# Five weight places in the second sweep, first projections back to back, fetched rows' products last in a unit

## The chip, the cores and the metric

The kernel runs on one core of one Trainium2 chip. The metric is the device time of one execution in microseconds; before the change the median of three runs is 1904.34 us (1901.85 to 1908.06).

## What is computed

One decoder block over 256 tokens of width 2048, in float32, with one layer:

```
h  = RMSNorm(x);  z = h @ w_in          # split into q, k, v, c_q, c_kv, k_r, gate_a, gate_b
y_a = window attention(q, k, v) @ w_a   # 16 heads, window 128
y_b = latent attention(c_q, c_kv, k_r) @ w_b
x  = x + (sigmoid(gate_a) * y_a + sigmoid(gate_b) * y_b) @ w_o
h2 = RMSNorm(x)
# expert mixer: per token 8 heads x 16 of 16384 experts, chosen by top-k of key scores
a  = h2 . u[expert];  w = gelu(a) * gate;  x = x + sum of w * v[expert]
out = RMSNorm(x)
```

`u` and `v` are tables of 16384 rows of 2048 floats (128 MB each).

## The kernel before

**Weights as pieces.** All weights, in the order in which they are used, are cut into pieces of at most 2048 floats per partition (1 MB); `plan` lists them, with `u` and `v` as the last 128 pieces each. `feed_hi` (L100) takes the next piece: it gets a place `raw` (three of them, in turn), lets SP start the transfer (L107), and lets ACT copy it to float32r, a rounded form (`whi`, L108). The function that it returns lets DVE make the remainder (`wlo` = `raw` - `whi`, L112). Two places each of `whi` and `wlo` follow. A matrix product is then summed on PE from the parts: high by high, high by low, low by high. `stream` keeps one piece ahead. SP issues its transfers in order, each when its `raw` place has been released by L112.

**Order of the work.** Up to the second sweep's beginning, a scheduler at compile time fills the engines' queues from the program and its dependences, so an instruction can stand earlier in a queue than it does in the program (POOL clears `vap`, L417, at 1.57 us). From `tc.manual_schedule()` (L945) on, the program's order is each engine's order.

**The start.** x is transposed and loaded in four parts; `make_x` (L206) makes `xc`, the high and low parts of x times gain, by ACT and DVE, one of 16 column blocks after the other. `nblock` (L159) multiplies row-wise: for every k three matmuls for each of two token halves. First comes `c_q` (512 columns, 96 matmuls, L242), with `make_x` called in groups of four blocks by `ahead_x`; then the norm of x: eight squares with sums on ACT (L248), a chain of small steps for `r1c`, two multiplications by the identity (`dg`, L255), and two products with ones on PE (L256), whose copy is `r1`. Then `c_kv` with `k_r` (320 columns, 96 matmuls, L376), written out with the factor `r1c` by `rows_out`.

**The u sweep.** Tokens are split: 192 (TD) get all 16384 experts by dense products, 64 (TG) get only their 128 experts each, whose rows are fetched. Per unit j of 128 (L948): 16 matmuls with `whi` (L952), in some units four products of one-hot matrices for the gates (L958, 48 such groups), then 16 matmuls with `wlo` (L981). Meanwhile ACT copies the last unit's PSUM (L902), makes the next `whi`, and applies GELU; DVE multiplies finished rows by their gates (L962), adds the PSUM parts (L905), makes the next `wlo` (L112), multiplies gate blocks (L979) and makes one-hots (L940).

**Fetched rows.** `gathered` (L844) is a generator of 130 steps. A step of the first 64 lets POOL fetch 128 rows of `u` by index (an indirect DMA of 1 MB, L828) into one of two places `urow`, and lets DVE multiply the row before by `h_nat` and sum it (L852, 2048 elements). Then one step for GELU, and 64 steps that fetch rows of `v` into three places `vrow` and add them, weighted, into `h_nat` (L865). A fetch waits until the product that read its place is done. `gather_to(goal)` runs steps up to a number: 54 (GU) of them are spread over the units of the u sweep after the routing is done (unit JR), the other 76 over the v sweep.

**The v sweep (the second sweep of 128 pieces).** For every piece n (L1036): 12 matmuls with `whi` (L1050 to L1052) and 8 with `wlo` (L1033), all 512 columns wide, into the eight PSUM banks, from stationary columns `wc` that ACT and DVE prepare for two pieces at a time (L873, L875, L876). `take(1)` at its top feeds the next piece, so that its `wlo` stands on DVE ahead of the step of `gathered` at the bottom. In pieces 80 to 103 SP also loads x and the last gain in 12 parts of 256 KB (L1044).

Of the kernel before, what the change touches and what calls it, by code (L numbers as in the profile page):

```python
# [8 lines left out]
F32 = mybir.dt.float32  # L9
# [56 lines left out]
def block(tc, a, out):  # L66
# [23 lines left out]

    plan, fed, ready = [], [0], []
    AHEAD = 1

    def planned(src):
# [3 lines left out]
    def feed_hi():  # L100
        src = plan[fed[0]]
        per, cols = src.shape[1], src.shape[2]
        m = per * cols
        raw = ring.tile([P, 2048], F32, name="raw", bufs=3)[:, :m]
        hi = ring.tile([P, 2048], F32R, name="whi", bufs=2)[:, :m]
        lo = ring.tile([P, 2048], F32R, name="wlo", bufs=2)[:, :m]
        sync.dma_start(raw.rearrange("p (k c) -> p k c", k=per), src)  # L107
        act.activation(hi, raw, AF.Copy)  # L108
        fed[0] += 1

        def rest():
            vec.tensor_tensor(lo, raw, hi.bitcast(F32), op=OP.subtract)  # L112
            ready.append([(hi[:, k * cols:(k + 1) * cols], lo[:, k * cols:(k + 1) * cols]) for k in range(per)])

        return rest
# [42 lines left out]

    def nblock(pss, nk, act_c, ahead=None):  # L159
        for k in range(nk):  # L160
            if ahead and k % 4 == 0:
                ahead(k // 4)
            wh, wl = next(wts)
            for c, ps in enumerate(pss):
                cs = slice(c * P, (c + 1) * P)
                pe.matmul(ps, act_c[:, k, 0, cs], wh, start=k == 0, stop=False)  # L166
                pe.matmul(ps, act_c[:, k, 0, cs], wl, start=False, stop=False)  # L167
                pe.matmul(ps, act_c[:, k, 1, cs], wh, start=False, stop=k == nk - 1)  # L168
# [19 lines left out]
    def acc_tile():  # L188
        accs[0] += 1
        return ps_acc.tile([P, 512], F32, name="acc", bufs=4)  # L190
# [12 lines left out]
    def load_x(k0, k1):  # L203
        sync.dma_start(xT[:, k0:k1, :], a["xT"][:, k0:k1, :])

    def make_x(k0, k1):  # L206
        for k in range(k0, k1):
            act.activation(xc[:, k, 0], xT[:, k], AF.Copy, scale=gm[:, k:k + 1])
            vec.scalar_tensor_tensor(xc[:, k, 1], xT[:, k], gm[:, k:k + 1], xc[:, k, 0].bitcast(F32),
                                     op0=OP.mult, op1=OP.subtract)  # L210
# [4 lines left out]
    ss = s0.tile([P, 2], F32, name="ss")  # L215
    tmp1 = s0.tile([P, 2], F32, name="tmp1")

    def ahead_x(q):
        if q == 0:
            return  # L220
        if q < 3:
            make_x(4 * q + 4, 4 * q + 8)


    idle = s0.tile([P, 512], mybir.dt.bfloat16, name="idle")
# [8 lines left out]
    make_x(2, 4)  # L234
    feed_hi()()
    load_x(4, 8)
    make_x(4, 8)
    feed_hi()()
    load_x(8, 12)
    load_x(12, 16)  # L240
    pss_cq = [acc_tile() for _ in range(2)]
    nblock(pss_cq, KO, xc, ahead=ahead_x)  # L242
    for c in range(2):
        sync.dma_start(xn[:, c], a["x_rows"][c])
    for c in range(2):
        for i in range(4):
            d = slice(i * 512, (i + 1) * 512)
            act.activation(xn[:, c, d], xn[:, c, d], AF.Square, accum_out=sp4[:, c, i:i + 1])  # L248
    vec.tensor_reduce(ss, sp4, axis=AX.X, op=OP.add)
    vec.tensor_scalar(ss, ss, 1.0 / D, EPS, op0=OP.mult, op1=OP.add)  # L250
    rsqrt(r1c, ss, tmp1)
    dg = s0.tile([P, 2, P], F32, name="dg")
    ps = acc_tile()
    for c in range(2):
        vec.tensor_scalar(dg[:, c], ident, r1c[:, c:c + 1], None, op0=OP.mult)  # L255
        pe.matmul(ps[:, c * P:(c + 1) * P], ones, dg[:, c], start=True, stop=True)  # L256
    act.activation(r1, ps[:, :T], AF.Copy)
    st.close()


# [79 lines left out]
    def rows_proj(cols, dst):  # L340
        pss = [acc_tile() for _ in range(2)]
        nblock([p[:, :cols] for p in pss], KO, xc)
        rows_out(dst, pss, cols)
# [29 lines left out]
                                     op0=OP.mult, op1=OP.mult)  # L373

    rows_out(cq, pss_cq, 512)
    rows_proj(320, ckr)  # L376
    norm_rows(cq, 512, gcq)
    norm_rows(ckr, 256, gckv)
    for c in range(2):
# [507 lines left out]
    def gather_to(goal):  # L887
        nonlocal gdone
        while gdone < STEPS and gdone <= goal:
            next(gat, None)  # L890
            gdone += 1
# [56 lines left out]
    for j in range(NJ):  # L948
        ps = acc_tile()
        ws = ready.pop(0)  # L950
        for k, (wh, wl) in enumerate(ws):
            pe.matmul(ps[:, :2 * TD], wh, hc[:, k].rearrange("p a t -> p (a t)"), start=k == 0, stop=False)  # L952
        fresh = []
        if hot and hot[0][0] + 2 <= j:
            G = ps_g.tile([P, 4, P], F32, name="G", bufs=2)
            _, o1, o2 = hot.pop(0)
            for q in range(4):
                pe.matmul(G[:, q], o1[:, q], o2[:, q], start=True, stop=True)  # L958
            fresh.append(G)
        while prods:  # L960
            bj, ge = prods.pop(0)
            vec.tensor_tensor(bj, bj, ge, op=OP.mult)  # L962
        add = evict(*last) if last else None
        ready_lo = feed_hi()
        old = gelus[:]
        gelus.clear()
        if add:
            add()
        work.pull(1.5)
        if JR is not None:  # L970
            gather_to((j - JR) * GU / (NJ - JR))
        rest = []
        while grids:
            rest += finish_gates(grids.pop(0))
        for g in old:
            finish_unit(*g)
        ready_lo()
        for bh, gv in rest:
            vec.tensor_tensor(bh, bh, gv, op=OP.mult)  # L979
        for k, (wh, wl) in enumerate(ws):  # L980
            pe.matmul(ps[:, :TD], wl, hc[:, k, 0], start=False, stop=k == KO - 1)  # L981
        last = (j, ps)
        grids += fresh
        if j == 0:
            scores(*behind)
            work.add(routing())
            qs.close()
            xs.close()
            b1 = bs.enter_context(tc.tile_pool(name="b1", bufs=1))
            B.append(b1.tile([P, NJ // 2, TD], F32, name="B0"))  # L990
        if JR is None and not work.gens:
            JR = j
            rt.close()
            b2 = bs.enter_context(tc.tile_pool(name="b2", bufs=1))
            B.append(b2.tile([P, NJ // 2, TD], F32, name="B1"))
            ps_g = hs.enter_context(tc.tile_pool(name="ps_g", bufs=1, space=PSUM))
        if JR is None:
            continue
        if groups < NG and groups * (NJ - 8 - JR) < (j + 1 - JR) * NG:
            hot.append((j, *one_hots(4 * groups)))  # L1000
            groups += 1
        if j == NJ - 2:
            assert not grids
            assert done == TD and not hot
            gs.close()
            wcp = bs.enter_context(tc.tile_pool(name="wcp", bufs=1, reuse_waits="tile"))
            wcs = [take_w(0)]
# [28 lines left out]
    for n in range(NJ - 2):  # L1036
# [16 lines left out]
        add_to(0, S[:1], vl, turn=accs[0])  # L1053
        add_to(1, S[2:], vl, turn=accs[0])
        gather_to(GU + (n + 1) * (STEPS - GU) / (NJ - 8))
        if n == NJ - 5:
            assert gdone == STEPS
            act.activation(x2[LO, 3], h_nat[HI], AF.Copy)
            vec.tensor_tensor(x2[LO, 1], x2[LO, 1], h_nat[LO], op=OP.add)
# [149 lines left out]
```

## Time and profile before

| | before |
|---|---|
| median of three runs | 1904.34 us |
| profiled execution | 1913.5 us |
| its span, first to last instruction | 1911.7 us |
| PE busy | 1870.5 us (98%) |
| DVE busy | 1593.1 us (83%) |
| ACT busy | 1139.8 us (60%) |
| POOL busy | 349.9 us (18%) |
| moved by DMA | 526.16 MB, mean 275 GB/s |

PE is TensorE's matmul side, PEld its weight loads, DVE is VectorE, ACT is ScalarE, POOL is GpSimd, SP is the engine whose queue starts most transfers. A busy share counts the time in which an instruction of the engine runs. Matmuls overlap, so PE's busy time is not PE at its peak. The profiled execution is one, and its own time is 1913.5 us; the runs of the median were made without a profile.

### The profile page before, as it was taken

The numbers are of one execution on the slowest core, as the hardware profiler recorded it, in microseconds if no ns is written. First come the engines' busy times: TensorE is split into PE (matmuls) and PEld (weight loads), VectorE is DVE, ScalarE is ACT, GpSimd is POOL, SyncE is SP. The second block draws the span as 40 slices with busy tenths as digits, with TensorE's granted clock in tenths as the row PEclk, the third lists the DMA queues.
The fourth block names the chain that finished last, engine by engine and source line by source line (L and its number), as shares of the span: only waits on it lengthen the run. The fifth ranks groups of instructions, "written<-read, shape, count | busy, mean of one in ns | idle before, by whom it ended". The sixth has DMA issues, their size and how long they took to land.

```text
span 1911.7 us, 28123 instructions
## 1 busy us (share of the span) xinstructions
PE 1870.5 (98%) x10874; PEld 1680.9 (88%) x10874; DVE 1593.1 (83%) x2277; ACT 1139.8 (60%) x1754; POOL 349.9 (18%) x192
## 2 busy tenths in 40 slices
PE   8999999999999999999999999999999999999996
PEld 6888888888888999999999999998788788887885
DVE  5768878658679799998899999998888898888887
ACT  7655766545555455555999998855444444444444
POOL 0000000000000000515243334333322123112210
PEclk9999999999999999999999999999999999999998
DMA  7554444455555566667798898889999999999983
GB/s 275 191 174 151 143 162 141 160 192 180 207 203 185 176 216 231 227 229 274 295 346 345 345 350 338 324 335 356 373 374 359 386 385 364 387 395 381 399 328 127
DMA packets 77910, 526.16 MB, mean 275 GB/s; under 512 B 9168, under 2 KB 11472, under 8 KB 15568
## 3 DMA queue, kind: packets, MB, share of 16 engines
q1 hardware_dynamic: 59344, 390.14, 56.6%
q0 software_dynamic: 18432, 134.23, 17.3%
q8 instruction: 85, 1.39, 0.3%
q14 instruction: 49, 0.40, 0.1%
HBM read 520.14 MB, written 4.19 MB: 274 GB/s over the span
## 4 chain that ended last, share of the span: by engine, by line
PE 60%; issue 16%; POOL 8%; DVE 6%; DMA 5%; ACT 5%; SPq 0%; POOLq 0%; DVEq 0%; ACTq 0%
PE acc L146 15%; PE o L1033 8%; PE acc L952 8%; POOL urow L828 8%; PE acc L151 7%; PE acc L981 5%; PE o L1050 4%; DMA raw<-v 4%; PE o L1052 4%; PE o L1051 4%; DVE wlo L112 3%; ACT whi L108 3%; PE acc L167 1%; PE acc L168 1%; PE acc L166 1%
## 5 line engine op out<-in xcount | busy, mean ns | idle before, releaser
L112 DVE TENSOR_TENSOR wlo<-raw,whi 128x2048 fp32r<-128x2048 f32 (+2 forms) x363 | 827.0, 2279 | 216.4 <-ACT whi L108 212.7
L108 ACT ACTIVATE whi<-raw 128x2048 fp32r<-128x2048 f32 (+2 forms) x363 | 688.6, 1897 | 450.3 <-DMA raw<-v 238.9
L952 PE MATMUL acc<-hc,whi 128*128 128x384 f32 x2048 | 382.8, 339 | 0.0
L952 PEld LDWEIGHTS acc<-hc,whi 128*128 128x128 f32 x2048 | 353.2, 189 | 0.0
L981 PE MATMUL acc<-hc,wlo 128*128 128x192 f32 x2048 | 252.9, 275 | 4.8 <-DVE wlo L112 4.8
L1033 PE MATMUL o<-wlo,wc 128*128 128x512 f32 x1020 | 252.5, 390 | 1.5 <-DVE wlo L112 1.5
L981 PEld LDWEIGHTS acc<-hc,wlo 128*128 128x128 f32 x2048 | 244.8, 193 | 6.3 <-DVE wlo L112 6.3
L1033 PEld LDWEIGHTS o<-wlo,wc 128*128 128x128 f32 x1020 | 191.0, 188 | 42.6 <-DVE wlo L112 2.9
L146 PE MATMUL acc<-xc,whi 128*128 128x512 f32 x928 | 227.6, 394 | 0.0
L828 POOL DMA_INDIRECT urow<-u_rows,iv x64 | 167.0, 2610 | 314.1 <-DVE urow L852 311.1
L1050 PE MATMUL o<-whi,wc 128*128 128x512 f32 x504 | 197.5, 392 | 4.3 <-ACT whi L108 3.8
L146 PEld LDWEIGHTS acc<-xc,whi 128*128 128x128 f32 x928 | 170.3, 189 | 32.1
L1051 PE MATMUL o<-whi,wc 128*128 128x512 f32 x504 | 196.2, 389 | 0.0
L1052 PE MATMUL o<-whi,wc 128*128 128x512 f32 x504 | 196.2, 389 | 0.0
L828 POOL DMA_INDIRECT vrow<-v_rows,iv x64 | 116.1, 1814 | 347.3 <-DVE h_nat L865 317.3
L852 DVE SCALAR_TENSOR_TENSOR urow<-urow,h_nat 128x2048 f32<-128x2048 f32 x64 | 146.2, 2285 | 21.9 <-DMA urow<-u_rows,iv 21.9
L865 DVE SCALAR_TENSOR_TENSOR h_nat<-vrow,gg,h_nat 128x2048 f32<-128x2048 f32 x63 | 147.8, 2346 | 0.0
L721 POOL TENSOR_TENSOR cand<-tv 128x256 f32<-128x256 f32 x16 | 14.0, 891 | 730.4 <-DVE tv L714 633.4
L902 ACT ACTIVATE ge<-acc 128x192 f32<-128x192 f32 x128 | 41.4, 324 | 152.7 <-PE acc L981 150.4
L151 PEld LDWEIGHTS acc<-xc,wlo 128*128 128x128 f32 x928 | 119.2, 191 | 4.5
L151 PE MATMUL acc<-xc,wlo 128*128 128x256 f32 x928 | 121.2, 283 | 0.0
L1050 PEld LDWEIGHTS o<-whi,wc 128*128 128x128 f32 x504 | 94.6, 188 | 28.5 <-ACT whi L108 8.3
(329 smaller groups left out, 2254.8 us busy)
## 6 DMA issues: line engine op xcount, KB each, us to landing
raw<-u SPq DMA_DIRECT2D x128, 1024.0 KB, 5.1
raw<-v SPq DMA_DIRECT2D x128, 1024.0 KB, 8.2
raw<-w_ga SPq DMA_DIRECT2D x16, 1024.0 KB, 4.8
raw<-w_gb SPq DMA_DIRECT2D x16, 1024.0 KB, 4.8
raw<-w_o SPq DMA_DIRECT2D x16, 1024.0 KB, 4.9
raw<-w_pq SPq DMA_DIRECT2D x16, 1024.0 KB, 4.9
raw<-w_q SPq DMA_DIRECT2D x8, 1024.0 KB, 4.8
raw<-w_a SPq DMA_DIRECT2D x8, 1024.0 KB, 4.9
```

The lines of the kernel that those rows point to most:

```text
L108: act.activation(hi, raw, AF.Copy)
L112: vec.tensor_tensor(lo, raw, hi.bitcast(F32), op=OP.subtract)
L146: pe.matmul(ps, ws[k][0], act_c[:, k].rearrange("p a t -> p (a t)"), start=k == 0, stop=False)
L151: pe.matmul(ps[:, :T], ws[k][1], act_c[:, k, 0], start=False, stop=k == nk - 1)
L828: pool.indirect_dma_start(out=dst, out_offset=None, in_=table, in_offset=bass.IndirectOffsetOnAxis(ap=idx, axis=0))
L865: later(vec.scalar_tensor_tensor(h_nat, r, gg[:, i:i + 1], h_nat, op0=OP.mult, op1=OP.add))
L952: pe.matmul(ps[:, :2 * TD], wh, hc[:, k].rearrange("p a t -> p (a t)"), start=k == 0, stop=False)
L981: pe.matmul(ps[:, :TD], wl, hc[:, k, 0], start=False, stop=k == KO - 1)
L1033: pe.matmul(O[c][i], st_, v[:, i * 512:(i + 1) * 512], start=first and k == 0, stop=last and k == len(ss) - 1)
L1050: pe.matmul(O[0][i], S[0], vh[:, d], start=n == 0, stop=False)
L1051: pe.matmul(O[0][i], S[1], vh[:, d], start=False, stop=False)
L1052: pe.matmul(O[1][i], S[2], vh[:, d], start=n == 0, stop=False)
```

## The change

It does four things. In the start, `ahead_x` makes one column block of `xc` ahead of every k instead of four ahead of every fourth; the `c_kv` product runs directly behind the `c_q` product on PE, with the squares of the norm called in two groups at its k = 4 and k = 8, and L256 comes after it, into a PSUM tile of its own. In the u sweep the step of `gathered` moves from ahead of the next `wlo` to behind it and behind the gate products, not in the last unit, with its 54 steps spread over one unit less. In the v sweep, once all 64 products with `urow` are issued (`gdone > NS`), two of every five pieces (those whose number leaves 3 or 4 when divided by 5) use the two `urow` places as their `raw`; the others go on with the three of the ring.

```diff
--- before.py
+++ after.py
@@ -90,7 +90,7 @@
 
 
 
-    plan, fed, ready = [], [0], []
+    plan, fed, ready, spare = [], [0], [], []
     AHEAD = 1
 
     def planned(src):
@@ -101,7 +101,10 @@
         src = plan[fed[0]]
         per, cols = src.shape[1], src.shape[2]
         m = per * cols
-        raw = ring.tile([P, 2048], F32, name="raw", bufs=3)[:, :m]
+        if spare and fed[0] % 5 > 2:
+            raw = spare[0]()
+        else:
+            raw = ring.tile([P, 2048], F32, name="raw", bufs=3)[:, :m]
         hi = ring.tile([P, 2048], F32R, name="whi", bufs=2)[:, :m]
         lo = ring.tile([P, 2048], F32R, name="wlo", bufs=2)[:, :m]
         sync.dma_start(raw.rearrange("p (k c) -> p k c", k=per), src)
@@ -158,8 +161,8 @@
 
     def nblock(pss, nk, act_c, ahead=None):
         for k in range(nk):
-            if ahead and k % 4 == 0:
-                ahead(k // 4)
+            if ahead:
+                ahead(k)
             wh, wl = next(wts)
             for c, ps in enumerate(pss):
                 cs = slice(c * P, (c + 1) * P)
@@ -215,11 +218,14 @@
     ss = s0.tile([P, 2], F32, name="ss")
     tmp1 = s0.tile([P, 2], F32, name="tmp1")
 
-    def ahead_x(q):
-        if q == 0:
-            return
-        if q < 3:
-            make_x(4 * q + 4, 4 * q + 8)
+    def ahead_x(k):
+        if k + 6 < KO:
+            make_x(k + 6, k + 7)
+
+    def squares_x(c):
+        for i in range(4):
+            d = slice(i * 512, (i + 1) * 512)
+            act.activation(xn[:, c, d], xn[:, c, d], AF.Square, accum_out=sp4[:, c, i:i + 1])
 
 
     idle = s0.tile([P, 512], mybir.dt.bfloat16, name="idle")
@@ -234,27 +240,29 @@
     make_x(2, 4)
     feed_hi()()
     load_x(4, 8)
-    make_x(4, 8)
+    make_x(4, 6)
     feed_hi()()
     load_x(8, 12)
     load_x(12, 16)
+
     pss_cq = [acc_tile() for _ in range(2)]
     nblock(pss_cq, KO, xc, ahead=ahead_x)
     for c in range(2):
         sync.dma_start(xn[:, c], a["x_rows"][c])
-    for c in range(2):
-        for i in range(4):
-            d = slice(i * 512, (i + 1) * 512)
-            act.activation(xn[:, c, d], xn[:, c, d], AF.Square, accum_out=sp4[:, c, i:i + 1])
+    pss_ck = [acc_tile() for _ in range(2)]
+    psn = ExitStack()
+    ps_n = psn.enter_context(tc.tile_pool(name="ps_n", bufs=1, space=PSUM))
+    nblock([p[:, :320] for p in pss_ck], KO, xc, ahead=lambda k: squares_x(k // 4 - 1) if k in (4, 8) else None)
     vec.tensor_reduce(ss, sp4, axis=AX.X, op=OP.add)
     vec.tensor_scalar(ss, ss, 1.0 / D, EPS, op0=OP.mult, op1=OP.add)
     rsqrt(r1c, ss, tmp1)
     dg = s0.tile([P, 2, P], F32, name="dg")
-    ps = acc_tile()
+    ps = ps_n.tile([P, 512], F32, name="nacc")
     for c in range(2):
         vec.tensor_scalar(dg[:, c], ident, r1c[:, c:c + 1], None, op0=OP.mult)
         pe.matmul(ps[:, c * P:(c + 1) * P], ones, dg[:, c], start=True, stop=True)
     act.activation(r1, ps[:, :T], AF.Copy)
+    psn.close()
     st.close()
 
 
@@ -373,7 +381,7 @@
                                      op0=OP.mult, op1=OP.mult)
 
     rows_out(cq, pss_cq, 512)
-    rows_proj(320, ckr)
+    rows_out(ckr, pss_ck, 320)
     norm_rows(cq, 512, gcq)
     norm_rows(ckr, 256, gckv)
     for c in range(2):
@@ -967,8 +975,6 @@
         if add:
             add()
         work.pull(1.5)
-        if JR is not None:
-            gather_to((j - JR) * GU / (NJ - JR))
         rest = []
         while grids:
             rest += finish_gates(grids.pop(0))
@@ -977,6 +983,8 @@
         ready_lo()
         for bh, gv in rest:
             vec.tensor_tensor(bh, bh, gv, op=OP.mult)
+        if JR is not None and j < NJ - 1:
+            gather_to((j - JR) * GU / (NJ - 1 - JR))
         for k, (wh, wl) in enumerate(ws):
             pe.matmul(ps[:, :TD], wl, hc[:, k, 0], start=False, stop=k == KO - 1)
         last = (j, ps)
@@ -1053,6 +1061,9 @@
         add_to(0, S[:1], vl, turn=accs[0])
         add_to(1, S[2:], vl, turn=accs[0])
         gather_to(GU + (n + 1) * (STEPS - GU) / (NJ - 8))
+        if gdone > NS and not spare:
+
+            spare.append(lambda: ghp.tile([P, D], F32, name="urow", bufs=2))
         if n == NJ - 5:
             assert gdone == STEPS
             act.activation(x2[LO, 3], h_nat[HI], AF.Copy)
```

## Rows read from the trace of the kernel before

**Rows 1.** page, part 1: engine busy us (share) xinstructions

```profile
PE 1870.5 (98%) x10874; PEld 1680.9 (88%) x10874; DVE 1593.1 (83%) x2277; ACT 1139.8 (60%) x1754; POOL 349.9 (18%) x192
```

**Rows 2.** waits of the whole run: waiting <- releaser: us in total, times, longest us

```profile
PEld o L1050 <- ACT whi L108: 8.3, 11, 1.4
...
PEld acc L981 <- DVE wlo L112: 6.3, 5, 2.9
...
PE acc L256 <- DVE dg L255: 3.0, 1, 3.0
...
PEld acc L167 <- DVE wlo L112: 2.9, 3, 1.1
```

**Rows 3.** four windows: us, busy us (x count) by engine, granted clock, DMA share, GB/s

```profile
35.20:41.40 6.20, 6.18 (x24) 6.18 (x25) 2.77 (x8) 4.92 (x10) 0.95 (x3) 0.51 0.30 88
41.40:47.60 6.20, 6.20 (x45) 6.20 (x44) 3.36 (x9) 4.65 (x6) 0.00 (x0) 1.00 0.58 209
...
1277.10:1284.00 6.90, 6.90 (x28) 6.90 (x29) 6.34 (x10) 2.38 (x3) 0.70 (x1) 0.52 0.85 330
1284.00:1290.90 6.90, 6.90 (x52) 6.90 (x51) 5.97 (x6) 2.39 (x3) 3.67 (x2) 1.00 0.87 335
```

**Rows 4.** timeline of the start: start us, us, engine, line, operation

```profile
35.22 1.22 PE L256 MATMUL acc<-dg,ones 128*128 128x128 f32 x4 [2.98 <-DVE dg L255]
```

**Rows 5.** timeline late in the u sweep, same columns

```profile
1261.67 2.75 POOL L828 DMA_INDIRECT urow<-u_rows,iv  x1 [7.34 <-DVE urow L852]
...
1266.94 2.98 PE L952 MATMUL acc<-hc,whi 128*128 128x384 f32 x16
...
1267.37 1.92 ACT L108 ACTIVATE whi<-raw 128x2048 fp32r<-128x2048 f32 x1
...
1271.52 2.98 PE L952 MATMUL acc<-hc,whi 128*128 128x384 f32 x16
...
1272.48 2.29 DVE L852 SCALAR_TENSOR_TENSOR urow<-urow,h_nat 128x2048 f32<-128x2048 f32 x1 [2.79 <-DMA urow<-u_rows,iv]
...
1277.05 3.73 PE L981 MATMUL acc<-hc,wlo 128*128 128x192 f32 x16 [2.55 <-DVE wlo L112]
```

**Rows 6.** timeline in the v sweep: two fetches and the subtraction beside each

```profile
1604.75 1.08 POOL L828 DMA_INDIRECT vrow<-v_rows,iv  x1 [10.82 <-DVE h_nat L865]
1604.93 2.29 DVE L112 TENSOR_TENSOR wlo<-raw,whi 128x2048 fp32r<-128x2048 f32 x1
...
1609.39 2.29 DVE L112 TENSOR_TENSOR wlo<-raw,whi 128x2048 fp32r<-128x2048 f32 x1
1609.75 2.74 POOL L828 DMA_INDIRECT vrow<-v_rows,iv  x1 [3.92 <-DVE h_nat L865]
```

**Rows 7.** tile urow, 927 to 1300 us: duration ns min/median/max; DVE's wait; landing us

```profile
L828 POOL DMA_INDIRECT urow<-u_rows,iv x51: 2743/2745/2750, 925.3 to 1299.1; - x51
...
  DMA urow<-u_rows,iv: 14.1, 9
...
DMA to landing us min/median/max: 9.3/9.9/11.9
```

**Rows 8.** one window, gate stage of the u sweep, columns as in rows 3

```profile
927.00:1300.00 373.00, 367.93 (x2625) 366.09 (x2623) 350.45 (x446) 320.10 (x691) 136.43 (x51) 0.99 0.89 342
```

**Rows 9.** tile vrow, whole run: from issue to landing, us

```profile
DMA to landing us min/median/max: 6.7/10.8/18.9
```

**Rows 10.** three windows of the v sweep, columns as in rows 3

```profile
1500.00:1690.00 190.00, 190.00 (x840) 157.32 (x839) 165.59 (x111) 87.72 (x63) 46.66 (x26) 1.00 0.98 383
1690.00:1780.00 90.00, 87.52 (x382) 70.88 (x381) 75.29 (x50) 40.70 (x30) 21.68 (x12) 1.00 0.99 392
...
1377.00:1881.00 504.00, 499.97 (x2191) 409.88 (x2190) 426.69 (x291) 237.57 (x170) 112.91 (x63) 1.00 0.95 371
```

**Rows 11.** tile raw, 1377 to 1881 us: idle until the transfer (us, times); landing us

```profile
  DMA raw<-v: 209.3, 82
...
DMA to landing us min/median/max: 4.8/8.5/13.2
```

## The prediction

> **What bounds the kernel now.** I read the page's engine table first: TensorE (PE) is busy 1870.5 us, 98% of the span [rows 1]. Only the other 41 us can be won by moving work, plus whatever part of the busy time ran at the lower of its two clocks. So the second view is the list of waits, for PE and its weight loads alone [rows 2]: the reader is to see that four waits fit the four places the diff touches. PE waits 3.0 us once for `dg` (L256, start), its weight loads wait 6.3 us in five pieces for `wlo` in the u sweep (L981), and 8.3 us in eleven pieces for `whi` in the v sweep (L1050). [...] In 35.2 to 41.4 us it made 24 matmuls, in the next equal stretch 45; so 6.2 x (1 - 24/45) = 2.9 us went there. In 1277.1 to 1284.0 it made 28 against 52: 6.9 x (1 - 28/52) = 3.2 us. [...]
>
> **Part A, the first projections back to back.** Before, PE ends the `cq` block, and the norm of x (8 squares on ACT, then a chain of small DVE and ACT steps) reaches `dg` too late: PE idles 2.98 us before the first L256 matmul [rows 4]. After, the 96 matmuls of `ckr` come between. They need about 0.14 us each at full clock (45 in 6.2 us, [rows 3]), some 13 us, which covers the rest of the norm several times. Gain: 2.98 + 2.9 = 5.9 us. The squares are the same eight, now two groups of four behind ACT's weight copies; the copies must still be there in time, and a `ckr` piece lasts PE 24 x 0.14 = 3.4 us, in which ACT copies the next and DVE subtracts. For 2048 columns these take 1.92 us [rows 5] and 2.29 us [rows 6], so for 1280 an estimated 1.2 and 1.4 us: 0.8 us are left. Four squares of 512 columns ahead of one copy, by their 2048 columns about one copy of 1.92 us, would cost PE between 0 and 1.9 us each time. I take 0, because the squares ran before while ACT had nothing else to do, and their data are there by then; 1.9 stays for the range. Making `xc` one column block at a time costs the same instructions; the start waits for its weight transfers either way, so I book 0, with the 2.9 us of three short waits for `wlo` [rows 2] as the other end of what it could give.
>
> **Part B, the product of a fetched row goes last in a unit of the u sweep.** The row to look at is a stall from end to end [rows 5]. POOL starts a fetch at 1261.67. Its row is there only at 1272.48, 10.8 us later; until then DVE sits idle 2.79 us in front of the product, and behind the product, on the same queue, stands the `wlo` subtraction that PE needs. PE waits 2.55 us at 1277.05 and loses its clock. In the gate stage DVE waits for such rows 14.1 us in nine pieces [rows 7], and each leads towards a PE wait, because DVE has little to spare: 350.4 of 373 us busy [rows 8].
>
> Merely turning the order round would give less than it seems, since the queue is a cycle: the next unit's `wlo` stands behind this unit's product still. Two things change all the same. First, `wlo` comes 2.29 us earlier against the unit that needs it, about as long as the longest wait (2.9 us). Second, the fetch gets quicker. In the u sweep every fetch occupies POOL for 2.74 to 2.75 us and lands after 9.3 to 11.9 us [rows 7]. In the v sweep the shortest lands after 6.7 [rows 9]. The pair of rows at 1604.75 and 1609.75 shows why [rows 6]: both fetches are released by a product, but POOL needs 1.08 us where `wlo` begins 0.18 us after it, and 2.74 us where `wlo` began 0.36 us before; it then ends 0.8 us after `wlo` does. Today `wlo` directly follows each product, so each fetch that the product releases is held up, and by then the weight transfer that `wlo` releases is queued ahead of it. With the product last, short instructions follow it (one-hots, products, the PSUM add), and `wlo` a microsecond later. I expect about 6.7 to 7.5 us to landing. Three products in successive units without gate blocks leave 2 x 4.58 (1266.94 to 1271.52, [rows 5]) less the product's 2.29, that is 6.9 us, and units with gate blocks more; so most DVE waits end, and the others shrink to under a microsecond. The gain is at most 6.3 + 3.2 = 9.5 us; I take 8.5, because a fetch can still lose against a DVE instruction. The last unit has no product any more and the pace is 54 steps over one unit less: the product count is the same, at no cost.
>
> What the moved step is moved past: on DVE `wlo` and the gate products; on POOL the next fetch is issued with it, later in the unit, but relative to the product where it was; on SP the weight load that waits for `wlo`'s release goes out earlier. What DVE loses: between its PSUM add and the end of ACT's copy the product used to stand. ACT copies PSUM first, so that copy is there when the weight copy starts, at 1267.37; the weight copy ends at 1269.29 [rows 5]. Less 0.4 us for the add, DVE can idle 1.5 us per unit, where it is not behind anyway. I book 0 and make a rival of it.
>
> **Part C, two more places for weight pieces in the v sweep.** PE's pace without a stop is 190/840 = 0.226 us a matmul, 4.53 us a piece of 20; 504 us would hold 2228 matmuls and the row has 2191, so 37 x 0.226 = 8.4 us are lost [rows 10], which is the wait of [rows 2] by another way. The cause is ACT waiting for the transfer, 209.3 us in 82 pieces [rows 11]. With three places a piece has 3 x 4.53 = 13.6 us from issue to release, and uses 8.5 (landing, median) + 1.92 + 2.29 = 12.7. The slowest landing, 13.2 [rows 11], overruns by 3.8 us. With five places it has 22.6 us, which covers the slowest. The places are free only after all 64 products, about 17 pieces into the sweep (11 products at 76 steps per 120 pieces), and have to be filled while the DMA engines are nearly full, so the first stops stay. I take 6.5 of 8.4, with 1 and 8.4 as ends. POOL's fetches of v rows share the engines with up to two more pieces under way; they have three places and a product only every 1.6 pieces, 3 x 1.6 x 4.53 = 21.7 us a round against a slowest landing of 18.9 [rows 9], so 0 (each wait of DVE for one would delay a `wlo`, which has a piece's time to spare).
>
> Can the DMA engines deliver more? The rows say that they can a little: 371 GB/s over the stage, 383 where PE never stops, 392 where it does [rows 10]. [...]
>
> **Sum.** 5.9 + 8.5 + 6.5 = 20.9 us, against the profiled execution of 1913.5 us: 1892.6. That execution is 9.2 us above the median of the runs, 1904.34. If all of that lay in the waits that go, the median would end at 1892.6 too; if none, at 1883.4. I take the middle, **1888 us**. A difference under about 0.3% (5.7 us) can't be told from none here.
>
> **The rivals.**
> 1. *The fetch is not quicker*: a one-hot or a gate product on DVE blocks POOL until `wlo` has started, landing stays at 10 us, and the DVE wait merely moves. For it: all 51 fetches of the u sweep show the long form. Against: the short form at 1604.75, which is behind a product too and has `wlo` 0.18 us behind it. B falls away, on the median's scale 8.5 x 16.3/20.9 = 6.6: 1894.6. [...]
> 2. *The transfers are at their limit*, 392 GB/s with stalls: C gives nothing, 1893.
> 3. *A does not come out as written*: ahead of the sweep the order on the engines is chosen at compile time, and the squares may stand before a copy: 1888 + 4.6 = 1892.6, and up to 1.9 more.
> 4. *DVE becomes the bound of the second sweep* (slower): the 1.5 us of idle per unit. DVE has 373 - 350.4 = 22.6 us free in 75 units. With A and C still won (9.7 us), the time is equal where the idle comes in (22.6 + 9.7)/1.5 = 21 units; from 26 units on it is slower by over 5.7 us, and in half of them (38) it is 1904.3 - 9.7 + 57 - 22.6 = 1929. Against: a DVE that is behind finds the copy ready, so the idle heals itself.
>
> **How the numbers follow.** All three parts: 0.49. Rival 1: 0.17; rival 2: 0.13; rival 3: 0.10; two of them together (some 1899, within 0.3%): 0.07; rival 4: 0.04. The single rivals are still faster by over 5.7 us, so faster 0.89, same 0.07, slower 0.04. The range reaches from 1879 (all three at their upper ends, 5.9 + 9.5 + 8.4 = 23.8 off the median, and half of the start's 2.9) to 1898 (one part lost and a second at its low end).
>
> **What would show it.** Right: no wait before L256 and full clock from 32 to 47 us; POOL's `urow` fetches near 1.1 us and landing near 7; DVE's wait for `urow` and PE's for `wlo` at L981 near nothing; no half clock near 1277; in the v sweep PE near 2225 matmuls in 504 us and little wait for `whi`. Wrong: `urow` fetches still 2.74 us; PE waits at L981 in many units with DVE waiting for `whi` before L112; a v sweep with stops and 392 GB/s; a new wait of PE for `wlo` or `whi` before 50 us.

## The result and the profile after

The changed kernel takes **1893.97 us** (median of six runs, 1892.11 to 1894.44) beside 1905.76 us of the kernel before (six runs, 1901.85 to 1910.38): 11.8 us less. The ratio of the runs is 0.9922 with a 95% interval of 0.9904 to 0.9939 (the two medians alone give 0.9938). The forecast was 1888 us, with a range of 1879 to 1898: faster as forecast, by 11.8 us on the medians where 16.3 were forecast. The runs also lie closer together, within 2.3 us instead of 8.5. The profiled execution of the changed kernel took 1893.6 us, 19.9 less than that of the kernel before.

All lines behind the change have moved: L952 to L960, L981 to L989, L852 to L860, L828 to L836, L108 to L111, L112 to L115, L1050 to L1058. First the engines and the chain that ended last, from the page of the changed kernel:

```profile
PE 1861.2 (98%) x10874; PEld 1678.0 (89%) x10874; DVE 1592.0 (84%) x2277; ACT 1139.7 (60%) x1754; POOL 266.1 (14%) x192
...
PE 85%; DVE 5%; issue 4%; ACT 3%; DMA 2%; POOL 1%; SPq 0%; DVEq 0%; POOLq 0%; ACTq 0%
```

POOL was busy 349.9 us before [rows 1]: 84 us have gone. The pages give the fetches of u rows as 167.0 us before and 76.4 now, those of v rows as 116.1 and 121.5. Next PE's waits over the whole span (engine, line, what ended them: total us, times, longest):

```profile
PE tp L476 <- DVE lt L470: 5.5, 11, 0.8
PE o L1058 <- DVE ge L913: 2.5, 1, 2.5
PE acc L149 <- DVE qnT L435: 2.1, 1, 2.1
PE acc L170 <- DVE wlo L115: 1.7, 3, 0.7
...
PE tp L398 <- DVE ckr L380: 0.7, 1, 0.7
```

The wait for `dg`, those for `wlo` in the u sweep and nearly all of those for `whi` in the v sweep [rows 2] are gone. Two are new: 2.5 us at L1058, the first matmul of the v sweep, and 0.7 us at the transposes behind the first projections (L398). The fetches of the u sweep's late part answer to [rows 7]:

```profile
L836 POOL DMA_INDIRECT urow<-u_rows,iv x51: 936/1145/1149, 933.1 to 1289.6; - x51
...
  DMA urow<-u_rows,iv: 0.2, 1
```

1.145 us instead of 2.745, and DVE waits 0.2 us for a row where it waited 14.1. In the v sweep the two windows that answer to [rows 10] are these (PE, PEld, DVE, ACT and POOL busy us with instructions, granted clock, DMA share, GB/s):

```profile
1690.00:1780.00 90.00, 90.00 (x399) 74.53 (x398) 77.73 (x53) 41.85 (x30) 24.24 (x13) 1.00 1.00 399
1357.00:1861.00 504.00, 503.88 (x2223) 416.92 (x2222) 431.71 (x295) 240.37 (x171) 123.13 (x65) 1.00 0.95 375
```

2223 matmuls in 504 us where before had 2191, and in those 504 us ACT waits 8.0 us for pieces in the ring's three places and 7.7 us for those in the u rows' two; before it was 209.3 [rows 11]. Now the clock in five windows, two at the start and three around the seam of the two sweeps:

```profile
35.20:41.40 6.20, 6.11 (x41) 5.84 (x41) 3.83 (x14) 5.15 (x10) 1.68 (x3) 1.00 0.75 243
41.40:47.60 6.20, 6.20 (x45) 6.12 (x44) 5.95 (x17) 3.38 (x6) 0.25 (x1) 1.00 0.91 334
1284.00:1290.40 6.40, 6.40 (x49) 6.28 (x47) 5.64 (x9) 3.95 (x6) 1.53 (x2) 1.00 1.01 428
1290.40:1296.80 6.40, 3.93 (x11) 3.08 (x11) 5.19 (x8) 3.16 (x5) 0.27 (x1) 0.73 0.93 353
1296.80:1303.20 6.40, 6.40 (x30) 5.26 (x29) 6.40 (x5) 3.41 (x3) 2.74 (x1) 1.00 0.73 265
```

The two half-clock stretches of [rows 3] (granted 0.51 and 0.52 there) are gone (the granted clock is 1.00 from 35.2 to 47.6 us, and from the begin of the u sweep to 1290.4). In their place stands one behind the new wait: a mean of 0.73 over 1290.4 to 1296.8. In the kernel before, the v sweep began without a stop, and its first unit took 5.32 us; here it begins 2.47 us late and the unit takes 6.29. So the seam gives back 3.4 us.

### The profile page after: what moved, and what is told of

It reads as the page before. It is cut to its first block, busy times and chain, and to the rows that moved or that the text cites. A ratio compares the mean times of both kernels' runs of the same rounds, so it can differ in the third digit from the quotient of the medians.

```text
span 1891.8 us, 28116 instructions
## 1 busy us (share of the span) xinstructions
PE 1861.2 (98%) x10874; PEld 1678.0 (89%) x10874; DVE 1592.0 (84%) x2277; ACT 1139.7 (60%) x1754; POOL 266.1 (14%) x192
## 4 chain that ended last, share of the span: by engine, by line
PE 85%; DVE 5%; issue 4%; ACT 3%; DMA 2%; POOL 1%; SPq 0%; DVEq 0%; POOLq 0%; ACTq 0%
PE acc L960 18%; PE acc L149 15%; PE acc L989 11%; PE o L1041 11%; PE acc L154 8%; PE o L1058 5%; PE o L1060 5%; PE o L1059 5%; DVE wlo L115 3%; PE G L966 2%; ACT whi L111 2%; DMA urow<-u_rows,iv 1%; POOL urow L836 1%; PE acc L170 1%; PE acc L171 1%
## 5 line engine op out<-in xcount | busy, mean ns | idle before, releaser
L115 DVE TENSOR_TENSOR wlo<-raw,whi 128x2048 fp32r<-128x2048 f32 (+1 forms) x319 | 726.4, 2277 | 187.4 <-ACT whi L111 183.5
L111 ACT ACTIVATE whi<-raw 128x2048 fp32r<-128x2048 f32 (+1 forms) x319 | 604.3, 1894 | 333.8 <-PE o L1060 159.2
L960 PE MATMUL acc<-hc,whi 128*128 128x384 f32 x2048 | 381.4, 338 | 0.0
L960 PEld LDWEIGHTS acc<-hc,whi 128*128 128x128 f32 x2048 | 351.8, 188 | 0.0
L989 PE MATMUL acc<-hc,wlo 128*128 128x192 f32 x2048 | 250.6, 274 | 0.0
L989 PEld LDWEIGHTS acc<-hc,wlo 128*128 128x128 f32 x2048 | 243.5, 192 | 0.0
L1058 PE MATMUL o<-whi,wc 128*128 128x512 f32 x504 | 196.8, 391 | 2.6 <-DVE ge L913 2.5
L836 POOL DMA_INDIRECT vrow<-v_rows,iv x64 | 121.5, 1899 | 333.5 <-DVE h_nat L873 305.7
L860 DVE SCALAR_TENSOR_TENSOR urow<-urow,h_nat 128x2048 f32<-128x2048 f32 x64 | 146.1, 2284 | 4.9 <-DMA urow<-u_rows,iv 4.6
L111 ACT ACTIVATE whi<-urow 128x2048 fp32r<-128x2048 f32 x44 | 84.7, 1924 | 108.8 <-PE o L1060 101.1
L836 POOL DMA_INDIRECT urow<-u_rows,iv x64 | 76.4, 1194 | 395.1 <-DVE urow L860 272.1
L115 DVE TENSOR_TENSOR wlo<-urow,whi 128x2048 fp32r<-128x2048 f32 x44 | 100.7, 2289 | 31.6 <-ACT whi L111 31.6
L910 ACT ACTIVATE ge<-acc 128x192 f32<-128x192 f32 x128 | 41.3, 323 | 142.1 <-PE acc L989 136.3
```

What stands on the lines that cost most here:

```text
L836: pool.indirect_dma_start(out=dst, out_offset=None, in_=table, in_offset=bass.IndirectOffsetOnAxis(ap=idx, axis=0))
L1058: pe.matmul(O[0][i], S[0], vh[:, d], start=n == 0, stop=False)
```

## Experiments

Eleven kernels ran, in three sets; each set has its own runs of the kernel before (medians 1906.97, 1909.97 and 1907.97 us), and the ratios go against those.

**1 to 3. Each part alone**, the diff of the change cut to its hunks.

> The kernel before with part A alone (both first projections back to back, x prepared one tile at a time, the norm's sums in a PSUM pool of their own). Theory: A brings the first sweep forward by about 5 us, but it takes one tile fewer from the four accumulator places, and with that the second sweep begins on the very place that the last unit frees last: TensorE stops 1.5 to 2.5 us there and runs at the half clock after it, and some 3.4 us are given back; net -1.5 to -2 us on the profiled execution, so 1903 to 1905 on the median. Rival: the stop at the start of the second sweep is B's doing (the product now last in a unit); then there is no stop over 0.5 us here, and the net gain is the whole 5 us, about 1900.8.

> The kernel before with part B alone (the fetched row's product last in a unit, none in the last unit). Theory: the fetches take 0.9 to 1.2 us instead of 2.74, the product's waits for a fetched row in the first sweep's late part fall from 14 us to under 1, TensorE's stops at the wlo products there go; the second sweep begins as in the kernel before, with a stop under 0.5 us; -7 us in the first sweep of the profile, and -5 on the median (about 1900.5), since the waits that go were not the same in every execution. Rival: the 2.5 us stop and the half clock at the start of the second sweep come with B: then the first unit of the second sweep takes over 6 us here too and the gain is 3.5 us at most. Second rival: without C the quicker fetch changes nothing in the second sweep, so its waits for v stay at some 230 us on ScalarE; both theories share that.

> The kernel before with part C alone (two of five weight pieces of the second sweep go to the places of the fetched u rows). Theory: ScalarE's waits for a piece of v fall from 239 us to under 60, the second sweep takes 568 to 570 us instead of 577, -8 us in the profile and -5 to -6 on the median, about 1900. Rival: transfers are at their limit and the places only let them run ahead once: -1 us, 1904.

Measured: A 1904.6 us, ratio 0.9988 (0.9972 to 1.0004); B 1899.51, 0.9954 (0.9938 to 0.9970); C 1906.51, 0.9981 (0.9966 to 0.9997). The three changes in ratio add up to -0.77%, and the whole change has -0.78%, so no dependence of the parts on each other shows; each ratio is uncertain by some 0.16%, so one of a few us could hide. Of the 14.7 us that they make on 1907 us, B has 8.8, C 3.6 and A only 2.3, and A's interval takes in no change at all. B gave more than expected here. C missed: its median lies 6.5 us above the expected 1900, although ACT's waits for pieces did nearly go (15.5 us in the window of [rows 11]). This window of its trace answers to the third of [rows 10]:

```profile
1377.00:1881.00 504.00, 501.81 (x2206) 414.93 (x2205) 429.86 (x292) 238.40 (x170) 122.99 (x64) 1.00 0.95 374
```

PE made 15 matmuls more than before, worth 3.4 us at 0.226 us each, for 194 us less of ACT's waiting: most of that waiting had never reached PE. A's median lies within what was expected. Its own trace, the second slowest of its twelve runs, shows where some of its gain went; PE's waits from 664 us on, then DVE and PE at the seam:

```profile
PE acc L986 <- DVE wlo L112: 7.1, 6, 2.0
PE o L1055 <- DVE ge L910: 4.0, 1, 4.0
```

```profile
1303.01 2.29 DVE L112 TENSOR_TENSOR wlo<-raw,whi 128x2048 fp32r<-128x2048 f32 x1
1305.21 0.35 DVE L910 TENSOR_TENSOR ge<-acc,ge 128x192 f32<-128x192 f32 x1
...
1299.69 1.93 PE L986 MATMUL acc<-hc,wlo 128*128 128x192 f32 x16
1305.62 0.79 PE L1055 MATMUL o<-whi,wc 128*128 128x512 f32 x1 [4.00 <-DVE ge L910]
1306.21 0.63 PE L1056 MATMUL o<-whi,wc 128*128 128x512 f32 x1
```

PE has ended the last unit at 1301.6 and waits for that unit's addition (L910), which stands behind the product and `wlo` on DVE; the slow spacing of 0.43 us behind it is the half clock (granted 0.50 over 1305.6 to 1308.6). The 7.1 us for `wlo` ahead of the seam are 2.3 more than in the kernel before, though A changes no instruction of that stage. B alone, where the product is last in a unit, stopped only 1.0 us at the seam; the executions without A have 0 to 1.8 us of such waits there, the three with A and the old round 2.5 to 4.0. So the seam's stop comes with A, the part that is at work 1250 us earlier. A takes the norm's sums out of the four `acc` places, so one tile fewer is counted, and the round in which the v sweep takes over the places, `(i + accs[0]) % 4`, begins on the place that the last unit frees.

**4 and 5. The round one place later**, on the changed kernel and on part A alone:

```diff
-            i = (i + accs[0]) % 4
+            i = (i + accs[0] + 1) % 4
...
-        add_to(0, S[:1], vl, turn=accs[0])
-        add_to(1, S[2:], vl, turn=accs[0])
+        add_to(0, S[:1], vl, turn=accs[0] + 1)
+        add_to(1, S[2:], vl, turn=accs[0] + 1)
```

> The changed kernel, with the second sweep's round of the four accumulator places begun one place later, so that the place of the last unit comes last. Theory: the 2.5 us stop at the start of the second sweep falls under 0.5 us, the half clock behind it goes, the first unit takes under 5.4 us instead of 6.3, and the whole is 3 to 4 us under the changed kernel, about 1890.5. Rival: TensorE has to wait for the last unit's addition whatever the order (it frees the pool and not a place): the stop stays and so does the time, 1893.9.

> Part A alone, with the second sweep's round of the accumulator places begun one place later. Theory: the 4.0 us stop that A alone showed at the second sweep's start and the half clock behind it (2.3 us in its first unit) go; A then keeps its 5 us: 1900 to 1902. Rival: the start of the second sweep is not what takes A's gain (the time is made up at the next late transfer), 1904 to 1905 as A alone.

The stop goes in both, to 0.4 us in part A:

```profile
PE o L1055 <- DVE ge L910: 0.4, 1, 0.4
```

The whole change starts its v sweep straight behind the last matmul of the u sweep:

```profile
1289.23 1.93 PE L989 MATMUL acc<-hc,wlo 128*128 128x192 f32 x16
1291.00 0.41 PE L1058 MATMUL o<-whi,wc 128*128 128x512 f32 x1
1291.25 0.39 PE L1059 MATMUL o<-whi,wc 128*128 128x512 f32 x1
```

Part A then has 0.9976 (0.9964 to 0.9987) where it had 0.9988: about 4.6 us instead of 2.3, at 1905.48 us beside 1909.97, with intervals that overlap; the expected 1900 to 1902 were missed. The whole change has 1892.64 us, 0.9920 (0.9900 to 0.9941), no measurable step from 0.9922, and the expected 1890.5 were missed too. Its sweep does begin 1.9 us earlier, but the trace has four stops between 1321 and 1381 us that the changed kernel did not have, 2.4 us in all. In these two executions, what the seam gave was taken back within 90 us.

**6. Is it places that are short there?** The early part of the v sweep still has three places for weights, until the u rows are done. The edit gives the fetched v rows' places to two of five pieces from the first unit on (and the round one place later).

> The changed kernel with the round begun one place later and, from the second sweep's first unit on, two of five weight pieces in the places of the fetched v rows (not used until the first v row is fetched), then those of the u rows as in the changed kernel. Theory: with the stop at its start gone, the second sweep's first 17 units still have three places only and stop four times (2.4 us in the profile of the run with the later place); with places there at once they don't: 1889 to 1891. Rival: the transfers themselves are at their limit there, so that more places only move the stops: 1892 to 1893.

1892.18 us, 0.9908 (0.9892 to 0.9923), no measurable step from the last: the theory fell. Two stops stayed, of 1.7 and 1.5 us at 1317 and 1337. DVE ahead of the first:

```profile
1307.44 2.28 DVE L115 TENSOR_TENSOR wlo<-vrow,whi 128x2048 fp32r<-128x2048 f32 x1
1313.69 2.29 DVE L860 SCALAR_TENSOR_TENSOR urow<-urow,h_nat 128x2048 f32<-128x2048 f32 x1 [3.97 <-DMA urow<-u_rows,iv]
...
1316.45 2.28 DVE L115 TENSOR_TENSOR wlo<-raw,whi 128x2048 fp32r<-128x2048 f32 x1
```

It is the old stall in another place. The weights are there; DVE waits 3.97 us for a fetched u row, and `wlo` stands behind the product. The rows land later (12.8 us after issue at the median of 1292 to 1345 us, where the later round alone has 10.0); that pieces which run further ahead are the reason fits, but is not shown apart. Nor are all early stops of this kind: of the four with the later round alone two are at `wlo` behind such a row (0.57 and 0.66 us), but two are for `whi`, with ACT waiting for a piece. ACT and then PE at the first of these:

```profile
1331.61 1.92 ACT L111 ACTIVATE whi<-raw 128x2048 fp32r<-128x2048 f32 x1 [5.46 <-DMA raw<-v]
1333.58 0.50 PE L1058 MATMUL o<-whi,wc 128*128 128x512 f32 x1 [0.55 <-ACT whi L111]
```

**7. Rows a step further ahead.** The u rows that are fetched in the v sweep go to the three places of the v rows, one more in advance, and the weights get the u rows' two places almost at once (`fp` is None ahead of the v sweep):

```diff
-        u_rows, u_more = source(a["u_rows"], lambda: ghp.tile([P, D], F32, name="urow", bufs=2))
+        u_rows, u_more = source(a["u_rows"], lambda: (fp.tile([P, D], F32, name="vrow", bufs=3) if fp
+                                                         else ghp.tile([P, D], F32, name="urow", bufs=2)))
...
             u_more()
+            if fp and more:
+                u_more()
+                more = False
...
-        if gdone > NS and not spare:
+        if gdone > GU + 1 and not spare:
```

> The changed kernel with the round begun one place later, with the u rows that are fetched in the second sweep going to the three places of the v rows (one row further ahead), and with the u rows' two places taken for weight pieces from the sweep's first units on. Theory: the stops in the second sweep's first 17 units are VectorE's, which waits 4 to 9 us for a fetched u row there with wlo behind it in its order, and more places for weights only make that row later; with rows a step further ahead those waits fall under 2 us and the stops go: second sweep 580 to 582 us instead of 584.5, 1888 to 1890.5 on the median. Rival: the stops are the weight pieces' own (the transfer rate): they stay, 1892 to 1893.

1890.92 us (1887.55 to 1894.11), 0.9903 (0.9883 to 0.9923). It is the quickest median of all, 3.1 us under the changed kernel's, though the intervals overlap, and its ratio can't be told from that of places early (0.9908): what it shows is the stops, not a time. DVE waits for no u row in the first 110 us of the v sweep (6.7 us in four pieces with the later round alone), and PE's waits from the u sweep on are down to two:

```profile
PE o L1064 <- ACT whi L111: 0.4, 1, 0.4
PE G L972 <- ACT o L952: 0.2, 1, 0.2
```

That the rows end the stops, and not the early places, rests on places early, which has such places too and kept two stops; it is one execution of each.

**8 and 9. What makes the fetch slow.** On the kernel before, only the call that issues the product was moved: ahead of the one short addition that stood before it (8), and to the head of the unit, ahead of two short operations (9). Each unit still has `wlo` behind the product.

> The kernel before with the fetched row's product one step earlier in its unit: ahead of the 0.35 us addition instead of directly ahead of wlo, and nothing else. Theory (B's gain is the fetch's own speed, which wlo beside it costs): with a short addition between product and wlo POOL's fetch has begun before wlo does, it takes about 1.1 us instead of 2.74, and the gain is nearly that of B alone, 1899 to 1902. Rival (what counts is that wlo no longer stands behind the product in a unit): the fetch may be quick or not, but wlo still comes after the product, TensorE stops at the wlo products as before, 1905 to 1907.

> The kernel before with the fetched row's product first in its unit, ahead of two short operations (0.3 us each) and then wlo; wlo still comes after the product within the unit. Theory: a fetch started before wlo runs through, one that wlo has overtaken waits until wlo ends (with no short operation between, 2.74 us; with one, 3.01): with two between it takes about 1.1 us in nearly all units, TensorE's stops at the wlo products go, and the gain is that of B alone (1898 to 1901 beside a before of 1907). Rival: the place at the end of the unit is what counts: fetch quick, stops as before, 1905 to 1908.

The first missed; the second held, its median 0.9 us above the expected range. With one short addition between, the fetches took 3.010 us (median of 50) and nothing was gained: 1907.86 us, 0.9995 (0.9982 to 1.0007). One of them, with DVE around it:

```profile
1166.82 0.08 DVE L852 DVE_READ_ACCUMULATOR urow<-urow,h_nat 128x1 f32 x1
1166.82 0.35 DVE L905 TENSOR_TENSOR ge<-acc,ge 128x192 f32<-128x192 f32 x1
1167.09 2.28 DVE L112 TENSOR_TENSOR wlo<-raw,whi 128x2048 fp32r<-128x2048 f32 x1
...
1167.17 3.01 POOL L828 DMA_INDIRECT urow<-u_rows,iv  x1 [6.83 <-DVE ge L905]
```

POOL begins 0.35 us after the product's last instruction started, and `wlo` is 0.08 us ahead of it. The fetch ends at 1170.18, 0.81 us after `wlo` does (1169.37). In [rows 6] the held fetch ends 0.81 us behind `wlo` too (1612.49 and 1611.68). That fits a fetch that waits the whole `wlo` through and then does its work, which is the author's reading of these two pairs; what would hold it up is not shown. With two short operations ahead of `wlo` the fetches take 0.936 us, and the u sweep has no stop:

```profile
L828 POOL DMA_INDIRECT urow<-u_rows,iv x50: 936/936/938, 932.8 to 1288.7; - x50
...
DMA to landing us min/median/max: 7.4/8.0/9.3
```

1901.89 us, 0.9962 (0.9947 to 0.9977), within the interval of B alone, though `wlo` follows the product in each unit: the place at the end of the unit is not what counts, but that the fetch gets away first. This execution's v sweep, without the two more places, had ten waits of PE, 4.9 us.

**10. The change without C.**

> The changed kernel without part C (three places for the weight pieces throughout). Theory (C is worth 1 to 4 us of the median, since in most executions most of TensorE's stops in the second sweep are gone once the fetches are quick): 1895 to 1898. Rival (the 8 us by which the second sweep got shorter in the profile are C's): 1901 to 1902.

1897.87 us, 0.9947 (0.9932 to 0.9962), within what was expected: C is worth 0.25% of 1907, 4.8 us, on top of A and B, and 3.6 alone. The intervals with and without C overlap a little (0.9904 to 0.9939 is the whole change). The stop at the seam, 2.6 us, is here too.

**11. The kernel before once more.**

> The kernel before once more, for a second profiled execution. Theory: the stops of TensorE in the late part of the first sweep (4.8 us in three stops in the first profile) and in the second sweep (8 stops, 5.3 us) are not the same in each execution; here they add up to other sums, by 2 us or more, at other places. Rival: they are the schedule's own: the same stops within 0.5 us.

This execution took 1903.8 us, 9.7 less than the first. PE's waits from the u sweep on, in the second profile and then in the first:

```profile
PE acc L981 <- DVE wlo L112: 4.6, 4, 1.4
PE o L1033 <- DVE wlo L112: 1.1, 2, 0.8
PE o L1050 <- DVE ge L905: 0.9, 1, 0.9
PE o L1050 <- ACT whi L108: 0.6, 2, 0.3
```

```profile
PE acc L981 <- DVE wlo L112: 4.8, 3, 2.5
PE o L1050 <- ACT whi L108: 3.8, 7, 1.0
PE o L1033 <- DVE wlo L112: 1.5, 2, 1.3
PE o L1050 <- DVE ge L905: 0.4, 1, 0.4
```

Half of the expectation held: in the v sweep 5.7 us became 2.6, those for `whi` nearly vanish; in the u sweep the stops differ in place and size, but their sum, 4.8 and 4.6 us, is the same. What differs there is the clock. It was 0.52 in 1277.1 to 1284.0 us of the first execution [rows 3]; the second has no slow stretch in its u sweep, here around the same place:

```profile
1270.00:1300.00 30.00, 28.73 (x203) 28.41 (x203) 28.64 (x31) 14.85 (x19) 10.97 (x4) 1.00 0.95 368
```

The same goes for the start. All six executions without A have the wait for `dg` (2.98 to 2.99 us, 4.46 in product first), but the clock fell behind it in four of them only. The window 35.2 to 41.4 of the second profile, of B alone and of product between, to be read beside the first of [rows 3]:

```profile
35.20:41.40 6.20, 5.09 (x26) 5.09 (x27) 3.85 (x16) 5.06 (x10) 0.95 (x3) 0.72 0.21 84
35.20:41.40 6.20, 6.12 (x43) 6.12 (x44) 2.93 (x10) 6.17 (x12) 0.95 (x3) 1.00 0.33 97
35.20:41.40 6.20, 6.04 (x42) 6.04 (x43) 2.94 (x10) 6.17 (x12) 0.96 (x3) 1.00 0.33 98
```

The stages of the thirteen profiled executions side by side (us; start of the u sweep's and the v sweep's first matmul, and PE's last one):

| kernel | u sweep begins | u sweep, with the seam | v sweep to PE's end |
|---|---|---|---|
| before, first and second profile | 664.9, 663.2 | 640.0, 637.1 | 590.6, 585.5 |
| changed | 659.9 | 633.0 | 582.6 |
| A alone | 660.0 | 645.6 | 587.0 |
| B alone | 660.8 | 634.0 | 584.3 |
| C alone | 664.6 | 643.6 | 587.3 |
| changed, round one later | 660.3 | 630.7 | 584.5 |
| A alone, round one later | 658.8 | 638.0 | 588.8 |
| places early | 661.1 | 630.4 | 584.2 |
| rows ahead | 659.7 | 631.1 | 581.8 |
| product between | 660.9 | 637.6 | 586.6 |
| product first | 665.0 | 630.4 | 592.8 |
| changed, without C | 658.4 | 633.6 | 585.5 |

## Why the prediction was right or wrong

**The sum** took one profiled execution of the kernel before as the measure, saw that it lay 9.2 us over the median, and took the middle between two readings. The table shows that this execution was slow in just the stages to be changed: the second profile of the same kernel is 9.7 us shorter, 1.7 of them ahead of the u sweep, 2.9 in it and 5.1 in the v sweep. The first two go with slow stretches of the clock (granted 0.51 and 0.52 [rows 3]) that the second execution has in part (0.72) or not at all (1.00), the last with fewer stops. So most of the 9.2 us lay in what goes, and the upper reading (1892.6, if all of it did) was nearer to the 1893.97 measured. By the ratio of the runs the gain is 14.9 us (11.6 to 18.3), by their medians 11.8; 16.3 lies above both but within the interval. That the total came so near is in part luck: on the median's scale the parts were booked at 4.6, 6.6 and 5.1 us and measured alone at 2.3, 8.8 and 3.6, so B's surplus covers over half of what A and C lack. Why the changed kernel's six runs lie closer together is not shown; rows ahead, with the fewest stops, spreads over 6.6 us.

**Part A**, 5.9 us in the profile and 4.6 on the median: the wait and the slow stretch went as said, and no matmul of the `ckr` block waited for a piece in any of the seven executions with A, so rival 3 did not come in. Without A the u sweep begins at 663.2 us on the mean of six executions, with A at 659.7 (seven): 3.5 us, not 5.9. The term that was too large is the slow stretch, 2.9 us, booked in full from one execution. That the stretch goes with the wait was the author's estimate, and no run shows it as a rule: in B alone and product between, where the wait had no slow stretch behind it (granted 1.00 over 35.2 to 41.4 us), the u sweep begins at 660.8 and 660.9 us, only about 1 us later than with A; 0.7 us are the new wait at L398, and the rest stays open. Then the seam took something back: 3.4 us in the changed kernel's trace, some 2.3 on the median in A alone (2.3 won, 4.6 with the round one place later), which is within the noise. This step was not in the list at all: the prediction counted the steps that A moves and not the tile that it takes out of a shared round. "What it removes" has to include counters.

**Part B**, 8.5 us in the profile and 6.6 on the median; measured 8.8 (0.9954, which is 5.7 to 11.8). The mechanism was right to the rows in the changed kernel: fetches at 1.1 us, 0.2 us of waiting for `urow`, no half clock near 1277 (B alone still waited 3.8 us for rows, and its PE 1.4 us once for `wlo`). Of the two reasons that the prediction gives, the second is enough by itself: product first has the quick fetch without the earlier `wlo`, and its gain is the same within the noise. And the 3.2 us of half clock in this term (granted 0.52 [rows 3]) were again those of one execution. The landing fell to 8.2 us at the median (B alone) and not to 6.7 to 7.5, and that was enough. Rival 1, that a one-hot or a gate product lets `wlo` overtake the fetch all the same, did not come in, but it was nearer than its 0.17 says: with one short operation between, it is what happens (product between). A fetch beside a `wlo` that had started first took 2.74 us in the kernel before [rows 6] and 3.01 in product between. A fetch that started first did not hold `wlo` up, as far as POOL's spans, which the profile gives only roughly, can say: in the changed kernel a fetch ran from 1289.59 to 1290.67, `wlo` began in the middle of it, at 1290.31, and took its usual 2.28 us (timeline of VectorE, then of POOL):

```profile
1290.31 2.28 DVE L115 TENSOR_TENSOR wlo<-raw,whi 128x2048 fp32r<-128x2048 f32 x1
...
1289.59 1.08 POOL L836 DMA_INDIRECT urow<-u_rows,iv  x1 [4.87 <-DVE urow L860]
```

That the last unit has no product, "at no cost", held: B alone stops 1.0 us at the seam, the kernel before 0.4 and 0.9.

**Part C**, 6.5 us in the profile and 5.1 on the median, between ends of 1 and 8.4; measured 3.6 alone (0.6 to 6.5) and 4.8 on top of the others. The term was sized from the stops of one execution; the other one of the same kernel has less than half of them (the v sweep's lines L1033 and L1050 add up to 2.6 us against 5.7). The cause named, ACT's 209.3 us of waiting for pieces, is far larger than what PE lost by it, as C alone shows. And the v sweep's early stops, which the prediction left standing as a shortage of places, are in good part DVE's waits for fetched u rows; more places alone did nothing for them (places early). Rival 2, the transfers at their limit, did not come in: 399 GB/s in 1690 to 1780 us, where before had 392 and stops [rows 10].

**Rival 4**, DVE as the bound of the u sweep (the prediction says second sweep, but its 75 units are the u sweep's): no sign, PE has no stop from 660 us to the seam.

What stays open: why the second sweep's stops vary so much between executions of one kernel, and why the clock falls behind a wait in one execution and not behind the same wait in another; no run here held either fixed.

## What to carry to other kernels

When an edit takes a tile out of a rotating pool, look for everything that counts on the rotation, however late in the kernel: here a norm at 47 us decided which accumulator was asked for first at 1291 us. A stall that goes at one place is a gain only if the next queue has room; what was left here was mostly a fetched row with the weight's subtraction queued behind it, and the stops went when the row was fetched a step earlier and not when the weights got more room, though neither moved the time clear of the noise. And before a term is sized from stops, profile the kernel before a second time: stops, and the slow stretches behind them, that come and go between executions are worth their mean and not what one profile shows.

## What the runs showed of the hardware

An indirect fetch on POOL that started 0.08 us after a 2.28 us subtraction of VectorE ended 0.81 us behind it, at 3.01 us (product between); one that started 0.18 us ahead of such a subtraction took 1.08 us [rows 6], although the subtraction then ran beside it, at its own usual length of 2.29 us. The transfers of this one core moved 399 GB/s over 90 us at a stretch (changed kernel, 1690 to 1780 us). In windows of 1 us from 30 to 1890 us the granted clock was 1.00 in 1840 and 0.50 in 14 of 1860 in the first execution of the kernel before, and 1.00 in 1842 and 0.50 in 13 in the changed kernel; the other six and five lie between. And here a wait of PE did not fix what its clock did next: behind the same wait of 2.98 to 2.99 us for `dg` the granted clock over 35.2 to 41.4 us was 0.51 and twice 0.72 in three executions and 1.00 in two; behind a wait of 2.1 us for `qnT`, which all thirteen have near 100 us, it was 0.91 over 100 to 120 us in six and 1.00 in seven.
